# Attention between projections: TensorE's instructions queued in the order of the source

## The chip, the cores and the metric

The kernel runs on one core of a Trainium2 chip. A core has a matrix engine (TensorE, "PE" in the profile, with its weight loads listed apart as "PEld"), three engines for element-wise work (VectorE or DVE, ScalarE or ACT, GpSimd or POOL), a sync engine that issues transfers (SP) and 16 DMA engines. Each engine works through a queue of its own, and semaphores hold an instruction until what it needs is there. The metric is the time of one execution on the device, in microseconds (us). Lower is better.

## What is computed

One decoder layer over 1024 tokens of width 1024, in float32. What matters here is its first part: a projection of the normalized input feeds three groups of heads, of which the second is a "stick-breaking" attention with 8 heads of 64.

```python
hn = rms_norm(h, norm1_g[i])
proj = hn @ w_in[i]
a_b, a_c, a_h, q, k, v, c_u, c_v = jnp.split(proj, split_idx, axis=-1)
y_a = a_b * short_conv(a_c * a_h, conv_w[i])
q = rms_norm(q.reshape(bsz, s_len, ATTN_HEADS, HEAD_DIM), q_norm_g[i])
k = rms_norm(k.reshape(bsz, s_len, ATTN_HEADS, HEAD_DIM), k_norm_g[i])
y_b = stick_breaking_attention(q, k, v).reshape(bsz, s_len, ATTN_W)
...
h = h + jnp.concatenate([y_a, y_b, y_c], axis=-1) @ w_out[i]
```

and in the attention, for each block of 128 queries:

```python
z = jnp.einsum('bqhd,bkhd->bhqk', qi, kj) * scale
log_beta = jax.nn.log_sigmoid(z)
log_rem = jnp.where(causal, jax.nn.log_sigmoid(-z), 0.0)
suffix = lax.cumsum(log_rem, axis=3, reverse=True) - log_rem
weights = jnp.where(causal, jnp.exp(log_beta + suffix), 0.0)
o = jnp.einsum('bhqk,bkhd->bqhd', weights, vj)
```

A large feed-forward part and a gated embedding follow; they take most of the kernel's time, and the change does not touch them.

## The kernel before

**Precision.** A float32 product is made of three matmuls: each operand is split into a high part (a cast on ACT) and a low part (a subtraction on DVE or POOL), in `split` (L135). `product` (L161) issues high by high, high by low and low by high.

**Stages around the change.** First the gating projection and the projection of the first pair of heads run "alone". Then four rounds each weave one pair's attention with other matrix work: pairs 0, 1 and 2 with the projections of pairs 1, 2 and 3, and pair 3 with most of the convolution's products. The rest of the convolution, the output product `o_ps` and the feed-forward part follow.

**Pieces.** All this is written as Python generators that emit one piece of work and then yield its size in units:

- `project(pr)` (L343) goes over 8 row blocks t. A block takes 4 pieces of 6 matmuls with 384 columns into a bank of `ps_mm` (two banks); each piece counts 18 units. Then q, k and v are read out of the bank: squares on ACT (L374), a sum on DVE (L377), a power on POOL (L174), the scaled q and k on DVE (L382), and v in two parts on ACT and DVE (L141, L142) into a V tile. After two blocks, 72 units later, `turn_qk` (L393) transposes q and k (8 units). For the last two blocks of a pair this comes when the generator ends (alone) or in the loop ahead of the next weave.
- `stick(hh, g)` (L435), two pieces for blocks t = 2g and 2g+1: the scores z of 128 queries against all keys up to them, in one bank of `ps_z` (two banks) for t under 4 and in two from there on; two sigmoids on ACT read each bank (L454, L455); a scan over the row on DVE (L459) and a product with its result on DVE or POOL (L462) give the weights. A piece counts 2(t+1)+10 units.
- `gather(hh, g)` (L469): `turn(j)` transposes the weights of two key blocks for both query blocks (up to 4 transposes into a bank of `ps_tr`, 18 or 16 units), which ACT casts and DVE subtracts into `wT_hi` and `wT_lo`; a later piece (8 units) multiplies them with V into `av` (L502), high and low parts in turn. A turn runs up to two ahead of its product.

`attention()` (L525) goes through 8 steps of each pair: head 0 with g = 0 to 3, head 1 with g = 3 to 0. The scores of the next step are always emitted ahead of the gather of this one.

**Weaving.** `weave` (L267) takes the next piece from whichever of the two generators lags behind its share: 834 units of attention to 608 of projection in the first round, 808 to 608 in the second and third, 782 to 829 units of convolution (pieces of 12 units, three matmuls of 512 columns) in the last.

**What sets the order.** The order of emission is not yet the order in the queues. The framework plans all engines when the kernel is built (`schedule_with_timeline_sim=True`, L1339): it plays the program through on estimated times, and each engine takes, among the instructions that the estimate has ready, the one emitted first. TensorE may so issue a later piece while an earlier one is not ready in the estimate. On the chip each queue is then worked off in the order planned. Some places already fix an order by hand, with `tc.issue_after`, for transfers (L293, L334) and for matmuls late in the kernel.

**Tiles.** The tiles of heads (`QS`, `KH`, `KL`, `V`, `q_lo`) come from a pool of 56 slots (L25, L44), which also holds the 32 tiles of the normalized input. A new tile takes a slot only when all readers of an old one are done.

Of the kernel before, what the change touches and what calls it, by code (L numbers as in the profile page):

```python
# [13 lines left out]
P = 128  # L14
# [18 lines left out]
def hybrid_block(ctx: ExitStack, tc: tile.TileContext, a: dict):  # L33
# [5 lines left out]
    nc = tc.nc  # L39
# [60 lines left out]
    ones = const.tile([P, P], F32, name="ones")  # L100
# [5 lines left out]
    ident_r = const.tile([P, P], F32R, name="ident")  # L106
    ident = ident_r.bitcast(F32)
# [4 lines left out]
    below = const.tile([P, P], F32R, name="below")  # L112
# [17 lines left out]
    gk = load_const("gk", [P, 1])  # L130


    last_hi, last_power = [None], [None]

    def split(src, hi, lo, scale=None, low=nc.vector):  # L135
# [25 lines left out]
    def product(ps, terms, first=True, last=True):  # L161


        for i, ((lh, ll), (rh, rl)) in enumerate(terms):
            nc.tensor.matmul(ps, lh, rh, start=first and i == 0, stop=False)  # L165
            nc.tensor.matmul(ps, lh, rl, start=False, stop=False)  # L166
            done = nc.tensor.matmul(ps, ll, rh, start=False, stop=last and i == len(terms) - 1)  # L167
        return done

    def cols(parts, sl):  # L170
# [14 lines left out]
    def mean_square(acc, s):  # L185


        ps = bank(ps_tr, "ms_ps")
        for t in range(4):
            nc.tensor.matmul(ps[:, 2 * t:2 * t + 2], acc[:, t * P:(t + 1) * P], ones[:, :2],  # L190
                             start=True, stop=True)
        ms = small.tile([P, 4], F32, tag=f"ms{s}", name=name("ms"), bufs=1)
        nc.vector.tensor_scalar(out=ms, in0=ps.rearrange("p (t two) -> p t two", two=2)[:, :4, 0],
                                scalar1=1.0 / D, scalar2=EPS, op0=ALU.mult, op1=ALU.add)
        r = small.tile([P, 4], F32, tag=f"r{s}", name=name("r"), bufs=1)
        power_mhalf(r, ms, 4)
        return ms, r

    def spread(r, R):

        diag = slot("diag", shape=(P, 4, P))
        nc.vector.tensor_tensor(
            out=diag, in0=ident.unsqueeze(1).broadcast_to([P, 4, P]),
            in1=r.unsqueeze(2).broadcast_to([P, 4, P]), op=ALU.mult)
        ps = bank(ps_tr, "R_ps")
        nc.tensor.matmul(ps, ones, diag.rearrange("p t c -> p (t c)"), start=True, stop=True)
        nc.scalar.copy(R, ps)
        return R

# [57 lines left out]
    def weave(first, first_total, second, second_total):  # L267


        done = [0, 0]  # L270
        while True:
            if done[0] * second_total <= done[1] * first_total:
                got = next(first, None)
                if got is None:
                    return
                done[0] += got
            else:
                done[1] += next(second, 1000)

# [113 lines left out]
    def turn_qk(head, t, qk):  # L393

        QS, KH, KL, _, low_q = head
        th = t // 4
        tr = bank(ps_tr, "qk_tr")
        for i in range(2):
            for j in range(2):
                o = j * 256 + i * P  # L400
                nc.tensor.transpose(tr[:, o:o + P], qk[:, i, j * P:(j + 1) * P], ident)
        ws = slice((t % 4 - 1) * P, (t % 4 + 1) * P)

        split(tr[:, :256], QS[0][th][:, ws], low_q[th][:, ws], scale=gq)
        nc.scalar.activation(KH[0][th][:, ws], tr[:, 256:], AF.Copy, scale=gk)
        for hh, own in enumerate((lo_p, hi_p)):
            nc.vector.scalar_tensor_tensor(out=KL[hh][th][own, ws], in0=tr[own, 256:],
                                           scalar=gk[own], in1=KH[0][th][own, ws],
                                           op0=ALU.mult, op1=ALU.subtract)
# [11 lines left out]
    def attend(pr):  # L421

        QS, KH, KL, V, _ = heads[pr]
# [11 lines left out]
        def stick(hh, g):  # L435
            weights[hh, g] = []
            for t in (2 * g, 2 * g + 1):
                W = (t + 1) * P
                th, ts = block(t)

                rem = at.tile([P, T], F32, tag="rem", name=name("rem"), bufs=3)
                wt = at.tile([P, T], F32, tag="wt", name=name("wt"), bufs=4)
                for kh in reversed(range(th + 1)):
                    n = min(HT, W - kh * HT)
                    ks = slice(kh * HT, kh * HT + n)
                    z = bank(ps_z, "z")[:, :n]
                    nc.tensor.matmul(z, QS[hh][th][:, ts], KH[hh][kh][:, :n],
                                     start=True, stop=False)
                    nc.tensor.matmul(z, QS[hh][th][:, ts], KL[hh][kh][:, :n],
                                     start=False, stop=kh < th)  # L450
                    if kh == th:

                        nc.tensor.matmul(z[:, n - P:], ident_r, below, start=False, stop=True)
                    nc.scalar.activation(rem[:, ks], z, AF.Sigmoid, scale=-HD ** -0.5)  # L454
                    last_act[0] = nc.scalar.activation(wt[:, ks], z, AF.Sigmoid,  # L455
                                                       scale=HD ** -0.5)

                back = rem[:, :W][:, ::-1]
                nc.vector.tensor_tensor_scan(out=back, data0=back, data1=back, initial=1.0,  # L459
                                             op0=ALU.mult, op1=ALU.bypass)  # L460
                on_vector = t in (3, 5, 7)
                done = (nc.vector if on_vector else nc.gpsimd).tensor_tensor(  # L462
                    out=wt[:, :W - 1], in0=wt[:, :W - 1], in1=rem[:, 1:W], op=ALU.mult)
                if not on_vector:
                    last_pool[0] = done
                weights[hh, g].append(wt)
                yield 2 * (t + 1) + 10

        def gather(hh, g):  # L469
            own = slice(hh * HD, (hh + 1) * HD)  # L470
            wts = weights.pop((hh, g))
            av_of[0] ^= 1
            av = av_bank[:, av_of[0] * 256:(av_of[0] + 1) * 256]

            def turn(j):

                tr = bank(ps_tr, "w_tr")
                n = 0
                parts = []
                for kb in (2 * j, 2 * j + 1):  # L480
                    first = 0 if kb <= 2 * g else 1
                    parts.append((kb, n, first))
                    for i in range(first, 2):
                        nc.tensor.transpose(tr[:, n:n + P], wts[i][:, kb * P:(kb + 1) * P], ident)  # L484
                        n += P
                hi, lo = tmp("wT_hi", F32R), tmp("wT_lo", F32R)
                split(tr[:, :n], hi[:, :n], lo[:, :n])
                return parts, hi, lo, n // P

            turned = []  # L490
            for j in range(-2, g + 1):
                if j + 2 <= g:
                    turned.append(turn(j + 2))
                    yield 2 * turned[-1][3] + 10
                if j < 0:
                    continue
                parts, hi, lo, _ = turned.pop(0)
                for kb, o, first in parts:
                    m = 256 - first * P
                    lhs = V[kb // 2][:, kb % 2, hh].rearrange("p two d -> p (two d)")  # L500
                    for part in (hi, lo):
                        nc.tensor.matmul(av[:, first * P:], lhs, part[:, o:o + m],  # L502
                                         start=kb == 0 and part is hi,
                                         stop=kb == 2 * g + 1 and part is lo)
# [51 lines left out]
    def gating():  # L556
# [26 lines left out]
        def turn_c(th, j, yc, y):  # L583
            tr = bank(ps_tr, "c_tr")
            for t in range(4):
                nc.tensor.transpose(tr[:, t * P:(t + 1) * P],
                                    yc[:, t].rearrange("p g e -> p (g e)"), ident)
# [93 lines left out]
    for n in range(KT):  # L681
# [5 lines left out]
        for h in range(2):  # L687
            ps = wide_bank("pp_ps")
# [234 lines left out]
    for h in range(2):  # L923
        for n in (0, 4, 1, 5, 2, 6, 3, 7):
# [35 lines left out]
            j = n % 4  # L960
# [382 lines left out]
```

## Time and profile before

| | |
|---|---|
| median of 3 runs | 1221.15 us (1217.46 to 1222.93) |
| the profiled execution | 1216.81 us |
| its span on the core | 1214.9 us |
| mean granted TensorE clock | 0.993 |
| first and last score matmul (z) | 108.9 and 394.3 us from the span's start |
| first and last projection matmul (`qkv_ps`) | 75.3 and 318.1 us |

In the profile a line such as "L455 ACT ACTIVATE wt<-z 128x512 f32<-128x512 f32 x12 | 7.4, 619 | 0.0" is a group: source line, engine, operation, output and input by the program's names, shapes, the count, then busy us in total, the mean ns of one, and the idle time of the engine just before them. A table of stretches lists, for each stretch of the span, its length, and for PE, PEld, DVE, ACT and POOL the busy us with the number of instructions; then the granted TensorE clock as a share, the DMA engines' busy share and GB/s. A timeline row has start, duration, engine, line, operation and, in square brackets, how long the engine had been idle and on whom it waited. Matmuls overlap in the array, so their start-to-start distance, not their duration, is the time that each costs.

### The profile page before, as it was taken

The page shows a single profiled execution, that of the slowest core. Times are in us where ns is not written, and L with a number is a line of the kernel's source. Part 1 is how long each engine was busy: PE and PEld are TensorE (multiplying, and loading weights), DVE is VectorE, ACT ScalarE, POOL GpSimd, SP SyncE. Part 2 cuts the span into 40 slices and gives each one's busy share as a digit, 9 for nine tenths or more (in the row PEclk, how much of TensorE's full clock was granted, in tenths as well). Part 3 has the DMA queues.
Part 4 walks back from the last instruction along what each step waited for, and adds up shares of the span by engine and source line. Part 5 has one row for each costly group of instructions (what it writes and reads, how often), then busy time and mean ns, then how long its engine had stood idle before and what let it go on. Part 6 is the DMA issues. An engine that isn't in the chain of part 4 may idle for free.

```text
span 1214.9 us, 17743 instructions
## 1 busy us (share of the span) xinstructions
PE 1191.8 (98%) x5852; PEld 1018.2 (84%) x5852; DVE 886.8 (73%) x1310; ACT 629.1 (52%) x1244; POOL 400.9 (33%) x408
## 2 busy tenths in 40 slices
PE   9999899999999999999999999999999999999997
PEld 7899899898988888888888888888888888888886
DVE  7846888988887657877878768787665556753597
ACT  7736767667764355744333333356443444546542
POOL 3324345365343312124453544421023301013412
PEclk9999999999999999999999999999999999999998
DMA  9602359999554786779999899778889985654857
GB/s 318 222 18 94 124 166 267 247 184 171 132 116 101 164 287 207 198 194 269 251 256 251 231 261 258 217 249 277 321 248 313 279 264 171 217 163 112 179 160 208
DMA packets 127964, 254.04 MB, mean 209 GB/s; under 512 B 14496, under 2 KB 22432, under 8 KB 127168
## 3 DMA queue, kind: packets, MB, share of 16 engines
q1 hardware_dynamic: 94992, 168.08, 41.8%
q0 software_dynamic: 27664, 57.05, 25.0%
q10 hardware_dynamic: 5216, 27.79, 6.4%
q8 instruction: 46, 0.75, 0.2%
q14 instruction: 46, 0.38, 0.1%
HBM read 192.30 MB, written 92.80 MB: 235 GB/s over the span
## 4 chain that ended last, share of the span: by engine, by line
PE 86%; DVE 5%; DMA 4%; POOL 1%; issue 1%; ACT 1%; SPq 0%; ACTq 0%; DVEq 0%; POOLq 0%
PE f_ps L812 25%; PE d_ps L812 25%; PE g_ps L812 6%; PE qkv_ps L165 3%; PE qkv_ps L166 3%; PE qkv_ps L167 3%; PE av L502 2%; PE w_tr L484 2%; DVE rem L459 1%; PE vu_ps L167 1%; PE vu_ps L166 1%; PE vu_ps L165 1%; PE o_ps L167 1%; PE o_ps L165 1%; PE o_ps L166 1%
## 5 line engine op out<-in xcount | busy, mean ns | idle before, releaser
L139 DVE TENSOR_TENSOR w_lo<-raw,w_hi 128x512 fp32r<-128x512 f32 x280 | 245.1, 879 | 88.1 <-ACT w_hi L138 86.4
L138 ACT CAST w_hi<-raw 128x512 fp32r<-128x512 f32 x280 | 171.9, 619 | 232.6 <-PE d_ps L812 112.6
L812 PE MATMUL f_ps<-hn_hi,w_hi 128*128 128x512 f32 x448 | 175.1, 392 | 0.0
L812 PE MATMUL d_ps<-f_hi,w_hi 128*128 128x512 f32 x448 | 174.8, 390 | 0.0
L812 PE MATMUL f_ps<-hn_lo,w_hi 128*128 128x512 f32 x448 | 174.7, 390 | 0.0
L812 PE MATMUL f_ps<-hn_hi,w_lo 128*128 128x512 f32 x448 | 174.5, 390 | 0.0
L812 PE MATMUL d_ps<-f_hi,w_lo 128*128 128x512 f32 x448 | 174.3, 389 | 0.0
L812 PE MATMUL d_ps<-f_lo,w_hi 128*128 128x512 f32 x448 | 174.3, 389 | 0.0
L459 DVE TENSOR_TENSOR_SCAN rem<-rem 128x128 f32<-128x128 f32 (+3 forms) x64 | 90.2, 1420 | 23.0 <-ACT rem L454 22.9
L812 PEld LDWEIGHTS f_ps<-hn_lo,w_hi 128*128 128x128 f32 x448 | 84.4, 188 | 17.9 <-issue 0.2
L812 PEld LDWEIGHTS f_ps<-hn_hi,w_hi 128*128 128x128 f32 x448 | 84.5, 189 | 17.6 <-issue 0.2
L812 PEld LDWEIGHTS f_ps<-hn_hi,w_lo 128*128 128x128 f32 x448 | 84.4, 188 | 17.7
L812 PEld LDWEIGHTS d_ps<-f_hi,w_hi 128*128 128x128 f32 x448 | 84.1, 188 | 17.7 <-issue 0.2
L812 PEld LDWEIGHTS d_ps<-f_lo,w_hi 128*128 128x128 f32 x448 | 84.1, 188 | 17.6 <-issue 0.2
L812 PEld LDWEIGHTS d_ps<-f_hi,w_lo 128*128 128x128 f32 x448 | 84.1, 188 | 17.5
L165 PE MATMUL qkv_ps<-whi,xn_hi 128*128 128x384 f32 x256 | 90.4, 353 | 0.1
L167 PE MATMUL qkv_ps<-whi,xn_lo 128*128 128x384 f32 x256 | 87.8, 343 | 0.0
L166 PE MATMUL qkv_ps<-wlo,xn_hi 128*128 128x384 f32 x256 | 87.6, 342 | 0.0
L139 DVE TENSOR_TENSOR f_lo<-raw,f_hi 128x512 fp32r<-128x512 f32 x112 | 77.0, 718 | 12.6 <-ACT f_hi L138 12.2
L138 ACT CAST f_hi<-raw 128x512 fp32r<-128x512 f32 x112 | 67.0, 620 | 28.9 <-DMA raw<-f_dram 25.9
L798 POOL TENSOR_TENSOR S<-S,sq 128x512 f32<-128x512 f32 x19 | 27.4, 1440 | 157.8 <-ACT sq L874 157.8
L174 POOL TENSOR_TENSOR rs<-ss,mhalf 128x4 f32<-128x4 f32 x32 | 40.1, 1253 | 83.1 <-DVE ss L377 83.1
(252 smaller groups left out, 2704.4 us busy)
## 6 DMA issues: line engine op xcount, KB each, us to landing
raw<-in_w_ff SPq DMA_DIRECT2D x148, 256.0 KB, 4.1
raw<-f_dram SPq DMA_DIRECT2D x112, 256.0 KB, 5.1
raw<-w_sums SPq DMA_DIRECT2D x64, 256.0 KB, 3.9
f_dram<-f SPq DMA_DIRECT2D x48, 256.0 KB, 4.0
f_dram<-t SPq DMA_DIRECT2D x48, 256.0 KB, 3.7
w_sums<-in_w_ff POOLq DMA_DIRECT2D x8, 1024.0 KB, 11.6
w_sums<-w_sums POOLq DMA_DIRECT2D x8, 1024.0 KB, 13.0
raw<-in_w_out SPq DMA_DIRECT2D x28, 256.0 KB, 3.9
```

The costliest lines, as they stand in the source:

```text
L138: last_hi[0] = nc.scalar.copy(hi, src)
L139: low.tensor_tensor(out=lo, in0=src, in1=hi, op=ALU.subtract)
L165: nc.tensor.matmul(ps, lh, rh, start=first and i == 0, stop=False)
L166: nc.tensor.matmul(ps, lh, rl, start=False, stop=False)
L167: done = nc.tensor.matmul(ps, ll, rh, start=False, stop=last and i == len(terms) - 1)
L174: last_power[0] = nc.gpsimd.tensor_tensor(out=out, in0=in_, in1=mhalf[:, :n], op=ALU.pow)
L459: nc.vector.tensor_tensor_scan(out=back, data0=back, data1=back, initial=1.0, op0=ALU.mult, op1=ALU.bypass)
L484: nc.tensor.transpose(tr[:, n:n + P], wts[i][:, kb * P:(kb + 1) * P], ident)
L502: nc.tensor.matmul(av[:, first * P:], lhs, part[:, o:o + m], start=kb == 0 and part is hi, stop=kb == 2 * g + 1 and part is lo)
L798: return eng.tensor_tensor(out=out, in0=x, in1=y, op=ALU.add)
L812: done = nc.tensor.matmul(bank, l, r, start=first and k == 0 and i == 0, stop=k == len(b) - 1 and i == 2, skip_group_check=True)
```

## The change

The matmuls and transposes of the front part go through two small helpers that remember the last one emitted, and each turn of `weave` runs inside `tc.issue_after` with it. That call adds an edge of issue order, without a semaphore: each instruction that the block emits on the same engine (TensorE) is placed in the queue behind the remembered one. It does not wait for the end of that instruction, and instructions on other engines get no edge. The helpers replace `nc.tensor.matmul` and `nc.tensor.transpose` in `product`, `mean_square`, `spread`, `turn_qk`, `stick`, `gather` and `turn_c`; only the pieces that `weave` takes are put in order.

```diff
+    last_mm = [None]
+
+    def matmul(*args, **kw):
+        last_mm[0] = nc.tensor.matmul(*args, **kw)
+        return last_mm[0]
+
+    def transpose(*args):
+        last_mm[0] = nc.tensor.transpose(*args)
...
         for i, ((lh, ll), (rh, rl)) in enumerate(terms):
-            nc.tensor.matmul(ps, lh, rh, start=first and i == 0, stop=False)
-            nc.tensor.matmul(ps, lh, rl, start=False, stop=False)
-            done = nc.tensor.matmul(ps, ll, rh, start=False, stop=last and i == len(terms) - 1)
+            matmul(ps, lh, rh, start=first and i == 0, stop=False)
+            matmul(ps, lh, rl, start=False, stop=False)
+            done = matmul(ps, ll, rh, start=False, stop=last and i == len(terms) - 1)
...
         done = [0, 0]
         while True:
-            if done[0] * second_total <= done[1] * first_total:
-                got = next(first, None)
-                if got is None:
-                    return
-                done[0] += got
-            else:
-                done[1] += next(second, 1000)
+            with tc.issue_after(last_mm[0].ins):
+                if done[0] * second_total <= done[1] * first_total:
+                    got = next(first, None)
+                    if got is None:
+                        return
+                    done[0] += got
+                else:
+                    done[1] += next(second, 1000)
...
-                nc.tensor.transpose(tr[:, o:o + P], qk[:, i, j * P:(j + 1) * P], ident)
+                transpose(tr[:, o:o + P], qk[:, i, j * P:(j + 1) * P], ident)
```

The other places change in the same way.

More of the change, by code (lines that the diff above doesn't have):

```diff
@@ L189, in mean_square @@
         for t in range(4):
-            nc.tensor.matmul(ps[:, 2 * t:2 * t + 2], acc[:, t * P:(t + 1) * P], ones[:, :2],
+            matmul(ps[:, 2 * t:2 * t + 2], acc[:, t * P:(t + 1) * P], ones[:, :2],
                              start=True, stop=True)
@@ L205, in spread @@
         ps = bank(ps_tr, "R_ps")
-        nc.tensor.matmul(ps, ones, diag.rearrange("p t c -> p (t c)"), start=True, stop=True)
+        matmul(ps, ones, diag.rearrange("p t c -> p (t c)"), start=True, stop=True)
         nc.scalar.copy(R, ps)
@@ L446, in stick @@
                     z = bank(ps_z, "z")[:, :n]
-                    nc.tensor.matmul(z, QS[hh][th][:, ts], KH[hh][kh][:, :n],
+                    matmul(z, QS[hh][th][:, ts], KH[hh][kh][:, :n],
                                      start=True, stop=False)
-                    nc.tensor.matmul(z, QS[hh][th][:, ts], KL[hh][kh][:, :n],
+                    matmul(z, QS[hh][th][:, ts], KL[hh][kh][:, :n],
                                      start=False, stop=kh < th)
                     if kh == th:
-                        nc.tensor.matmul(z[:, n - P:], ident_r, below, start=False, stop=True)
+                        matmul(z[:, n - P:], ident_r, below, start=False, stop=True)
                     nc.scalar.activation(rem[:, ks], z, AF.Sigmoid, scale=-HD ** -0.5)
@@ L483, in turn @@
                     for i in range(first, 2):
-                        nc.tensor.transpose(tr[:, n:n + P], wts[i][:, kb * P:(kb + 1) * P], ident)
+                        transpose(tr[:, n:n + P], wts[i][:, kb * P:(kb + 1) * P], ident)
                         n += P
@@ L501, in gather @@
                     for part in (hi, lo):
-                        nc.tensor.matmul(av[:, first * P:], lhs, part[:, o:o + m],
+                        matmul(av[:, first * P:], lhs, part[:, o:o + m],
                                          start=kb == 0 and part is hi,
@@ L585, in turn_c @@
             for t in range(4):
-                nc.tensor.transpose(tr[:, t * P:(t + 1) * P],
+                transpose(tr[:, t * P:(t + 1) * P],
                                     yc[:, t].rearrange("p g e -> p (g e)"), ident)
```

## The prediction

> **What bounds the kernel now.** I read the page's shares first, then tables of busy time by stretch over the part that the change touches, then the order of TensorE's matmuls there.
>
> ```profile
> span 1214.9 us, 17743 instructions
> PE 1191.8 (98%) x5852; PEld 1018.2 (84%) x5852; DVE 886.8 (73%) x1310; ACT 629.1 (52%) x1244; POOL 400.9 (33%) x408
> ```
>
> TensorE (PE) bounds the whole. Its busy time is modelled and covers short gaps, so for attention I read PEld, the weight loads: each matmul has its own, and where nothing is late they fill the time. In the table the columns are PE, PEld, DVE, ACT, POOL, granted clock. The first three rows are the three weaves with projections 1, 2 and 3, the fourth the weave with the convolution; then one packed stretch, then three poor ones.
>
> ```profile
> 111.00:175.50 64.50, 60.32 (x376) 57.15 (x375) 55.66 (x83) 44.98 (x115) 26.10 (x26) 0.97 0.48 162
> 175.50:245.50 70.00, 67.31 (x438) 64.59 (x437) 59.71 (x91) 49.03 (x125) 37.19 (x37) 0.98 0.89 235
> 245.50:318.50 73.00, 69.42 (x459) 66.20 (x458) 63.80 (x103) 51.64 (x131) 40.65 (x40) 1.00 0.83 160
> 318.50:408.50 90.00, 88.12 (x482) 73.55 (x480) 64.64 (x89) 45.44 (x103) 35.95 (x31) 1.00 0.60 131
> ...
> 151.00:175.50 24.50, 24.50 (x160) 24.22 (x160) 21.47 (x32) 14.95 (x37) 6.08 (x6) 0.95 0.52 178
> ...
> 140.00:151.00 11.00, 8.13 (x49) 6.15 (x48) 10.52 (x15) 9.91 (x24) 5.26 (x5) 0.97 0.01 1
> 210.00:221.00 11.00, 8.31 (x47) 6.76 (x46) 10.46 (x13) 9.24 (x24) 8.61 (x8) 0.89 0.83 144
> 279.00:289.00 10.00, 7.21 (x45) 5.30 (x44) 9.13 (x13) 9.36 (x23) 7.93 (x7) 1.00 0.81 138
> ```
>
> Weight loads fill 24.22 of 24.5 us in the packed stretch. In the first three weaves they are idle for 7.35, 5.41 and 6.80 us, 19.6 us in all, and the three poor stretches hold 4.85 + 4.24 + 4.70 = 13.8 us of it. There DVE is 91 to 96% busy and ACT 84 to 94%: attention runs alone and its vector work sets the pace. The projections' own matmuls in these stretches show why.
>
> ```profile
> 111.00:140.00 29.00, 21.78 (x114) 19.20 (x112) 3.47 (x9) 3.48 (x9) 1.00 0.63 209
> 140.00:151.00 11.00, 0.00 (x0) 0.01 (x1) 1.01 (x3) 0.64 (x2) 0.97 0.01 1
> 210.00:221.00 11.00, 1.57 (x5) 1.64 (x6) 1.03 (x3) 1.15 (x3) 0.89 0.83 144
> 279.00:289.00 10.00, 0.12 (x1) 0.15 (x2) 0.98 (x3) 0.76 (x2) 1.00 0.81 138
> ```
>
> The order is not the source's. Projection 1 races ahead (114 matmuls in 29 us) and then issues none in 11 us, with its first four row blocks done and the fifth not begun. Its next matmul starts at 151.06, right after two late evictions:
>
> ```profile
> 146.93 0.64 ACT L141 ACTIVATE V<-qkv_ps,r 128x128 fp32r<-128x128 f32 x2
> ...
> 150.26 0.61 DVE L142 SCALAR_TENSOR_TENSOR V<-qkv_ps,r,V 128x128 fp32r<-128x128 f32 x2
> ```
>
> Those free the two `ps_mm` banks. I read them as late because the V tiles need slots of the 56 that attention's first head still held; the rows show the lateness, not the slot.
>
> **The change part by part.** It adds no operation and no wait on another engine. It fixes TensorE's order in the four weaves: a piece's matmuls go in only after the last matmul of the piece emitted before. No DMA, ACT, DVE, POOL or SP instruction gets an edge.
>
> *Removed.* The first projection piece of row block 4 is then emitted about half-way through a weave (288 of 608 units), some 13 us of TensorE work behind the first head's last score. The blocked stretch should go. Ceiling: 19.6 us less the roughly 1% of idle that a packed stretch keeps, 2 us, gives 17.5. The convolution weave adds 90 - 88.12 = 1.9. The clock adds a little:
>
> ```profile
> 152.16 0.52 PE L165 MATMUL qkv_ps<-whi,xn_hi 128*128 128x384 f32 x1
> 152.48 0.52 PE L166 MATMUL qkv_ps<-wlo,xn_hi 128*128 128x384 f32 x1
> ...
> 155.14 0.33 PE L166 MATMUL qkv_ps<-wlo,xn_hi 128*128 128x384 f32 x1
> 155.32 0.33 PE L167 MATMUL qkv_ps<-whi,xn_lo 128*128 128x384 f32 x1
> ```
>
> After the poor stretch 384-column matmuls start 0.32 us apart instead of 0.17. A granted 0.95 over 24.5 us is 1.2 us, and 0.89 over 11 us is 1.2 us: 2.4 us. In all 17.5 + 1.9 + 2.4 = **21.8 us to gain**.
>
> *Added: waits with no filler.* What is queued behind a waiting matmul is now everything else on TensorE. To find the waits I lay out the source order (S: scores of one block, P: six projection matmuls, T: transposes, A: weights times V) and compare TensorE's own time between two dependent pieces with the chain on the other engines. Start-to-start times:
>
> ```profile
> 140.33 0.39 PE L449 MATMUL z<-KL,QS 128*128 128x512 f32 x1
> 140.56 0.22 PE L453 MATMUL z<-below,ident 128*128 128x128 f32 x1
> 140.62 0.45 PE L447 MATMUL z<-KH,QS 128*128 128x512 f32 x1
> ...
> 142.16 0.27 PE L502 MATMUL av<-wT_lo,V 128*128 128x256 f32 x1
> 142.27 0.28 PE L502 MATMUL av<-wT_hi,V 128*128 128x256 f32 x1
> 142.39 0.60 PE L401 MATMUL qk_tr<-ident,qk 128*128 128x128 f32 x4
> 142.75 0.36 PE L502 MATMUL av<-wT_lo,V 128*128 128x256 f32 x1
> ```
>
> That is 0.23 for 512 columns, 0.17 for 384 (above), 0.12 for 256, 0.06 for 128, and 0.36 for four transposes. So P is 1.04, S of block 7 0.97, S of block 6 0.86, A at most 0.47. The chains, from the second weave's groups (mean ns behind the comma):
>
> ```profile
> L455 ACT ACTIVATE wt<-z 128x512 f32<-128x512 f32 x12 | 7.4, 619 | 0.0
> L455 ACT ACTIVATE wt<-z 128x384 f32<-128x384 f32 x4 | 2.0, 509 | 0.0
> L138 ACT CAST wT_hi<-w_tr 128x512 fp32r<-128x512 f32 x12 | 7.0, 596 | 1.9 <-PE w_tr L484 1.9
> L459 DVE TENSOR_TENSOR_SCAN rem<-rem 128x1024 f32<-128x1024 f32 x2 | 5.0, 2475 | 0.0
> L459 DVE TENSOR_TENSOR_SCAN rem<-rem 128x768 f32<-128x768 f32 x2 | 3.5, 1756 | 2.3 <-ACT rem L454 2.3
> L459 DVE TENSOR_TENSOR_SCAN rem<-rem 128x512 f32<-128x512 f32 x2 | 2.4, 1204 | 0.0
> L139 DVE TENSOR_TENSOR wT_lo<-w_tr,wT_hi 128x512 fp32r<-128x512 f32 x12 | 7.9, 681 | 0.6 <-ACT wT_hi L138 0.4
> ```
>
> (1) Score banks. `ps_z` has two; each is read by two sigmoids. S6, P, S7: the second bank of S6 is free 0.41 + 0.2 + 2 x 0.51 + 2 x 0.62 = 2.9 us after S6 begins; TensorE wants it at 0.87 + 1.04 + 0.52 = 2.4. Wait 0.5, twice in a weave, and by the same working 0.25 for the S4, S5 pair: 1.5 us a weave if ACT does nothing else. ACT is 49.03 of 70 us busy, half of that not sigmoids, so a pair's 2.9 us meet some 1 us of other work: 5 us a weave. I take 3, nearer the free case.
>
> (2) First product of a gather. Each gather is emitted right behind a pair of scores, whose scans DVE then works through; the low parts of the first transposes stand behind the second scan. From S5's end: 0.2 + 1.24 + 1.76 + 0.68 + 0.2 = 4.1 us, and TensorE comes to A's low part after P, T, T, P, 2.8 us: wait 1.3. After S7: 4.8 against 4.2 or 4.3, 0.6 and 0.5. After S3: 3.4 against 2.45, 0.95. The rest about 0.4. That is 3.8 us a weave with an empty queue. DVE is 85% busy; one more operation of 0.7 us ahead at each of eight gathers makes it 9.4. I take 5, nearer the bound that has rows.
>
> (3) Last turn of q and k. The transposes of row blocks 6 and 7 are emitted between weaves, and the next piece stands behind them. Their chain:
>
> ```profile
> L374 ACT ACTIVATE qk_sq<-qkv_ps 128x256 f32<-128x256 f32 x8 | 3.1, 387 | 1.0 <-PE qkv_ps L167 0.9
> L377 DVE TENSOR_REDUCE ss<-qk_sq 128x4 f32<-128x260 f32 x9 | 3.7, 414 | 0.8 <-ACT qk_sq L374 0.8
> L382 DVE TENSOR_TENSOR qk<-qkv_ps,rs 128x256 f32<-128x256 f32 x8 | 3.3, 419 | 1.7 <-POOL rs L174 1.6
> ...
> L174 POOL TENSOR_TENSOR rs<-ss,mhalf 128x4 f32<-128x4 f32 x9 | 12.1, 1344 | 22.3 <-DVE ss L377 22.3
> ```
>
> 0.39 + 0.41 + 1.34 + 0.42 and 0.5 for the steps between is 3.1 us. Before the first weave nothing stands between: 3.1. Before the second there are 1.6 us of work: 1.5, of which 0.4 is already in (2). Later ones have 3.3 or more: none. Sum 4.2, between 2 and 6.
>
> Three weaves of 3 + 5 give 24 (16 to 43). The convolution weave has shorter filler pieces but a freer DVE (64.64 of 90): 4 to 8 by the same chains, less what its wider spacing covers; I take 3, from 1 to 8. **Added: 24 + 3 + 4.2 = 31 us** (19 to 57). The net is 31 - 22 = +9 us, with bounds -3 and +35.
>
> ```profile
> 141.82 0.39 PE L502 MATMUL av<-wT_lo,V 128*128 128x256 f32 x1 [0.41 <-DVE wT_lo L139]
> ...
> 150.29 1.11 PE L484 MATMUL w_tr<-ident,wt 128*128 128x128 f32 x4 [1.14 <-DVE KL L407]
> ```
>
> These are two of today's waits (in brackets, us). In the first nothing overtook the low product that stood waiting. [...] If matmuls could overtake, (1) to (3) would cost nothing and the net would be -22.
>
> The profiled execution took 1216.8 us, span 1214.9; the median shown is 4.3 above it. Plus 9 gives 1226 against the profile and **1230** against the median.
>
> **The rivals.** *Faster.* The low parts go ahead of the scans in DVE's queue, and ACT keeps the sigmoids together: (2) vanishes, (1) is 1.5 a weave, and what is added falls to 4.5 + 4.2 + 1 = 10: -12 us, 1209. For it: the plan orders ACT and DVE anew, and the three poor stretches are dear. Against it: the scans are emitted first, and DVE has 63.8 us of work for the third weave's 66 of weight loads. *Even.* Waits of 22 pay back just what is won: 1221. That the order does not move at all is excluded by the x0 row. *A DVE queue one deep.* The high ends hold for (1) and (2): 43 + 3 + 4 - 22 = +28, 1249. It decides from the point at which DVE's backlog lasts from one gather to the next; 59.71 of 70 us is near it. *Clock.* The new waits of a step fall close together and halve the clock as in the 152.16 row. Each such window costs 1.2 us by the granted clock; 12 pairs of long scores (four in each of three weaves) add 14 to the forecast: 1244. [...]
>
> **How the numbers follow.** Forecast, slower by 9: 0.45. Faster: 0.23. Even: 0.19. DVE queue: 0.09. Clock: 0.04. The likeliest case alone spans 1222 to 1240. To leave out no more than 2 in 10 the range reaches over most of the faster case and to the middle of the DVE one: **1207 to 1249**. A measurement here tells about 0.5%, 6 us, from no change. Faster by more than that 0.23; within it, the even case and the forecast's low edge, 0.27; slower 0.50.
>
> **What would show it.** Right on the removal: no stretch of 10 us in 111 to 318 without projection matmuls, weight loads evenly filled. Right on the cost: in the table of waits, products waiting for `wT_lo` and scores for `wt` go from a few to dozens, together over 15 us; a 2 to 3 us wait of the q and k transposes near 115 to 120. Wrong, if those stay under 10 us together (then 1209 to 1221), or if waits of projections for weights or V appear, for which I found no reason. After attention nothing should move.

## The result and the profile after

| | before | after |
|---|---|---|
| median | 1219.31 us (1216.32 to 1222.93, 4 runs) | 1268.55 us (1267.53 to 1270.20, 4 runs) |
| span of the profiled execution | 1214.9 us | 1267.7 us |
| mean granted TensorE clock | 0.993 | 0.981 |

The ratio is 1.0404, with an interval of 1.0369 to 1.0439: **slower by 4%**. One run in this document is left out of its median and ratio, one of the four of `e1_products_loose`, 1992.6 us at a granted clock of 0.555; as it was the profiled one, that experiment has times but no trace to compare. The shares on the page of the changed kernel:

```profile
PE 1210.2 (95%) x5852; PEld 1031.2 (81%) x5852; DVE 905.5 (71%) x1310; ACT 635.7 (50%) x1244; POOL 402.8 (32%) x408
```

Every engine has as many instructions as before; lines have moved down by some 11 (the scan L459 is L470, the product L462 is L473, the low part L139 is L149). To find the place of the 52.8 us I divided both spans at the same work: at the first projection matmul of pairs 1, 2 and 3 (the three weaves), at the end of the last projection (the convolution weave), and at the first output product `o_ps`. The table of stretches of the kernel before (length, then PE, PEld, DVE, ACT, POOL, granted clock, DMA share, GB/s):

```profile
115.70:183.90 68.20, 64.11 (x409) 61.19 (x410) 58.31 (x88) 47.56 (x121) 30.42 (x31) 0.97 0.53 167
183.90:251.60 67.70, 65.01 (x421) 62.28 (x420) 57.52 (x87) 47.17 (x120) 34.40 (x36) 0.97 0.88 236
251.60:318.10 66.50, 62.92 (x412) 59.80 (x411) 58.48 (x92) 45.83 (x117) 34.90 (x33) 1.00 0.86 167
318.10:420.30 102.20, 99.73 (x533) 82.89 (x532) 76.77 (x107) 52.09 (x116) 41.44 (x36) 1.00 0.60 130
```

and of the kernel after:

```profile
118.80:198.20 79.40, 69.49 (x420) 65.31 (x420) 61.56 (x85) 49.38 (x122) 29.64 (x31) 0.94 0.40 127
198.20:278.60 80.40, 70.38 (x424) 66.27 (x423) 62.00 (x88) 49.46 (x121) 33.10 (x33) 0.94 0.78 201
278.60:356.90 78.30, 67.45 (x409) 62.69 (x408) 62.85 (x91) 47.23 (x117) 34.22 (x34) 0.96 0.73 137
356.90:470.90 114.00, 102.55 (x533) 84.34 (x532) 81.78 (x112) 53.28 (x116) 43.81 (x36) 0.98 0.59 128
```

Behind the last row of each, 794.6 us are left before and 796.8 after. The three weaves grew from 202.4 to 238.1 us. In them weight loads were idle for 7.01 + 5.42 + 6.70 = 19.1 us before and are idle for 14.09 + 14.13 + 15.61 = 43.8 us after. Matmuls (the PE column, whose ends are modelled) were idle for 10.4 us and are idle for 30.8 us. About as many loads (1251 recorded, 1241 before) are also busy for longer, 194.3 us against 183.3, at a granted clock of 0.94, 0.94 and 0.96 where it had been 0.97, 0.97 and 1.00. Beside the forecast, whose terms I spread over the same places:

| place | forecast | measured |
|---|---|---|
| before the first weave | +3.1 | +3.1 |
| three weaves, loads idle (7.6 = 24 + 1.1 - 17.5) | +7.6 | +24.7 |
| three weaves, loads busy for longer (clock) | -2.4 | +11.0 |
| convolution weave up to `o_ps` | +1.1 | +11.8 |
| the rest | 0 | +2.2 |
| sum | +9.4 | +52.8 |

The removal did happen. The projection's own matmuls in a stretch that had none before:

```profile
139.00:151.00 12.00, 5.96 (x27) 4.73 (x26) 0.72 (x2) 1.16 (x3) 0.90 0.12 22
```

The longest gap between projection matmuls inside a weave is now 6.6 us, from 148.0 to 154.6, where three gaps of 9.8 to 11.7 us stood before.

What came instead of those stretches stands in the table of TensorE's waits after (who waited for whom: us in total, times, longest):

```profile
PE av L136 <- DVE wT_lo L149: 23.8, 25, 2.1
PE qk_tr L140 <- DVE qk L393: 5.4, 3, 3.8
PE o_ps L136 <- DVE cv_acc L672: 5.3, 1, 5.3
PE w_tr L140 <- DVE wT_lo L149: 4.0, 2, 2.4
PE qk_tr L140 <- DVE wT_lo L149: 2.8, 2, 2.2
...
PE z L136 <- ACT wt L466: 0.4, 1, 0.4
```

Waits of products for the low parts went from 1.6 us in 3 to 23.8 us in 25:

```profile
PE av L502 <- DVE wT_lo L139: 1.6, 3, 0.9
```

One of them in the timeline after (start, duration, engine, line, operation, idle time before). L470 is the scan, L473 the product of weights and scan, L149 the low part:

```profile
132.30 1.31 POOL L473 TENSOR_TENSOR wt<-wt,rem 128x639 f32<-128x639 f32 x1 [2.37 <-DVE rem L470]
132.59 2.64 DVE L470 TENSOR_TENSOR_SCAN rem<-rem 128x768 f32<-128x768 f32 x1 [0.22 <-ACT rem L465]
...
134.59 0.28 PE L136 MATMUL av<-wT_hi,V 128*128 128x256 f32 x1
135.34 0.96 DVE L473 TENSOR_TENSOR wt<-wt,rem 128x767 f32<-128x767 f32 x1
136.21 1.15 DVE L149 TENSOR_TENSOR wT_lo<-w_tr,wT_hi 128x512 fp32r<-128x512 f32 x2
136.95 0.39 PE L136 MATMUL av<-wT_lo,V 128*128 128x256 f32 x1 [2.08 <-DVE wT_lo L149]
...
137.83 0.49 PE L136 MATMUL qkv_ps<-whi,xn_hi 128*128 128x384 f32 x1
138.11 0.52 PE L136 MATMUL qkv_ps<-wlo,xn_hi 128*128 128x384 f32 x1
138.43 0.52 PE L136 MATMUL qkv_ps<-whi,xn_lo 128*128 128x384 f32 x1
```

The high part goes into the array at 134.59; the low part, next in the queue, stands until 136.95, because DVE first works off the scan and also the product L473. Projection matmuls that need neither stand behind it, and when they come they start 0.28 and 0.32 us apart, where 0.17 is usual: the granted clock from 139 to 141 us is 0.50.

The scan itself is long, 2.64 us. Before, the same scan of block 5 met no work on POOL:

```profile
131.03 1.59 POOL L462 TENSOR_TENSOR wt<-wt,rem 128x639 f32<-128x639 f32 x1
134.13 1.76 DVE L459 TENSOR_TENSOR_SCAN rem<-rem 128x768 f32<-128x768 f32 x1 [2.22 <-ACT rem L454]
...
143.28 2.29 DVE L459 TENSOR_TENSOR_SCAN rem<-rem 128x1024 f32<-128x1024 f32 x1
```

After, POOL's product runs from 132.30 to 133.61 and the scan, put down as started at 132.59, takes 0.88 us longer, for 1.02 us of overlap. With block 7 it is the same, 1.46 us longer than the scan of 2.29 above for an overlap of 1.61:

```profile
238.44 1.77 POOL L473 TENSOR_TENSOR wt<-wt,rem 128x895 f32<-128x895 f32 x1 [3.61 <-DVE rem L470]
238.60 3.75 DVE L470 TENSOR_TENSOR_SCAN rem<-rem 128x1024 f32<-128x1024 f32 x1 [0.34 <-ACT rem L465]
```

The groups by form show it as a mean over attention (110 to 470 us; busy us, mean ns), here for block 7, before:

```profile
L459 DVE TENSOR_TENSOR_SCAN rem<-rem 128x1024 f32<-128x1024 f32 x8 | 21.1, 2642 | 0.0
```

and after:

```profile
L470 DVE TENSOR_TENSOR_SCAN rem<-rem 128x1024 f32<-128x1024 f32 x8 | 28.4, 3547 | 2.1 <-ACT rem L465 2.1
```

### The profile page after: what moved, and what is told of

Its sections match the earlier page's. It is cut to its first block, busy times and chain, and to the rows that moved or that the text cites. A ratio compares the mean times of both kernels' runs of the same rounds, so it can differ in the third digit from the quotient of the medians.

```text
span 1267.7 us, 17707 instructions
## 1 busy us (share of the span) xinstructions
PE 1210.2 (95%) x5852; PEld 1031.2 (81%) x5852; DVE 905.5 (71%) x1310; ACT 635.7 (50%) x1244; POOL 402.8 (32%) x408
## 4 chain that ended last, share of the span: by engine, by line
PE 65%; DVE 2%; POOL 1%; DMA 1%; issue 0%; ACT 0%; POOLq 0%
PE f_ps L823 24%; PE d_ps L823 24%; PE o_ps L136 7%; PE g_ps L823 6%; PE cv_ps L136 2%; DVE rem L470 1%; PE ms_ps L898 1%; PE av L136 0%; DMA u_sums<-u_sums 0%; POOL cv_u L660 0%; PE z L136 0%; POOL cv_acc L670 0%; PE w_tr L140 0%; PE R_ps L913 0%; DMA u_sums<-in_w_ff 0%
## 5 line engine op out<-in xcount | busy, mean ns | idle before, releaser
L149 DVE TENSOR_TENSOR w_lo<-raw,w_hi 128x512 fp32r<-128x512 f32 x280 | 253.5, 909 | 90.2 <-ACT w_hi L148 84.2
L470 DVE TENSOR_TENSOR_SCAN rem<-rem 128x128 f32<-128x128 f32 (+3 forms) x64 | 101.9, 1603 | 25.4 <-ACT rem L465 24.9
L136 PE MATMUL qkv_ps<-whi,xn_hi 128*128 128x384 f32 x256 | 94.1, 368 | 0.0
L149 DVE TENSOR_TENSOR f_lo<-raw,f_hi 128x512 fp32r<-128x512 f32 x112 | 77.2, 719 | 10.1 <-ACT f_hi L148 9.7
L473 POOL TENSOR_TENSOR wt<-wt,rem 128x127 f32<-128x127 f32 (+4 forms) x40 | 50.6, 1269 | 89.0 <-DVE rem L470 56.5
```

The lines of the kernel that those rows point to most:

```text
L136: last_mm[0] = nc.tensor.matmul(*args, **kw)
L149: low.tensor_tensor(out=lo, in0=src, in1=hi, op=ALU.subtract)
```

## The experiments

The theory: each step's first weights-times-V products wait for low parts that stand behind DVE's scans, and everything queued behind them waits too. The rivals are the waits of the transposes of q and k; the lost clock by itself; and a cost of keeping order at all, wherever it is loosened. All ratios are against the kernel before, at 1217.1 to 1217.8 us in these batches.

| run | what | median us | ratio (interval) |
|---|---|---|---|
| e1_products_loose | products may be overtaken | 1232.29 | 1.0119 (1.0101 to 1.0137) |
| e2_qk_loose | q and k transposes may be overtaken | 1267.39 | 1.0408 (1.0389 to 1.0427) |
| e3_both_loose | both | 1230.19 | 1.0101 (1.0083 to 1.0120) |
| e4_rounds_0_2 | order in the three weaves alone | 1256.65 | 1.0321 (1.0302 to 1.0341) |
| e5_round_3 | order in the convolution weave alone | 1229.71 | 1.0091 (1.0060 to 1.0122) |
| e6_mult_on_pool | 24 products moved from DVE to POOL | 1246.24 | 1.0236 (1.0211 to 1.0261) |
| e7_window_3 | order with a window of 3 pieces | 1238.44 | 1.0169 (1.0142 to 1.0196) |
| e7_window_6 | window of 6 | 1214.13 | 0.9982 (0.9961 to 1.0002) |
| e7_window_12 | window of 12 | 1221.32 | 1.0032 (1.0016 to 1.0049) |
| e9_window_6_qk | window of 6, q and k loose | 1214.39 | 0.9971 (0.9957 to 0.9985) |
| e8_v_own_pool | kernel before, one V tile in slots of its own | 1215.77 | 0.9985 (0.9968 to 1.0002) |
| e10_filler | kernel after, 128 idle-time matmuls added | 1267.66 | 1.0400 (1.0367 to 1.0432) |

### Which matmuls hold the queue: e1, e2, e3

```diff
-                        matmul(av[:, first * P:], lhs, part[:, o:o + m],
+                        nc.tensor.matmul(av[:, first * P:], lhs, part[:, o:o + m],
```

A product that isn't remembered has nothing queued behind it.

> The weights-times-V products stay behind the piece ahead of them, but nothing is queued behind them any more. Theory A (products that wait for their low parts hold up everything behind them: 23.8 us of waits in the changed kernel, and half-rate clock after them): 1268 falls by 25 to 35, to 1233 to 1243, and the waits of products on wT_lo fall under 8 us. Theory B (DVE's backlog is the bound, the product is only where it shows): the waits move to transposes and scores, and the time stays at 1258 or above.

Measured: 1232.29, 36 us less than the kernel after with one word changed. That products hold up what is queued behind them carries most of the loss. How far their own waits fell isn't shown, as this run has no trace to compare; e3 below, where they are loose too, shows 8.3 us. The same for q and k:

```diff
-                transpose(tr[:, o:o + P], qk[:, i, j * P:(j + 1) * P], ident)
+                nc.tensor.transpose(tr[:, o:o + P], qk[:, i, j * P:(j + 1) * P], ident)
```

> Only the transposes of q and k are let go: nothing is queued behind them. Theory A: their waits in the changed kernel (5.4 on qk, 2.8 on wT_lo) and the half-rate clock after the first of them go, 6 to 10 us: 1259 to 1263. If the three us before the first weave are merely paid at the next piece: within 3 us of 1268.

Measured: 1267.39, 1 us less, within what the runs of either kernel spread. The wait has only moved on to the scores that need those transposes, as the table of waits of this run shows:

```profile
PE av L136 <- DVE wT_lo L149: 25.1, 27, 2.1
PE z L136 <- DVE QS L427: 7.4, 3, 3.5
```

With both loose:

> Products and q and k transposes both let go; scores, weight transposes and projections keep the source's order. Theory A: the gains add, 1225 to 1235. If the removal of the blocked stretches is worth what the prediction said (some 20 us), this order has few waits and could come below the kernel before: 1205 to 1219. Theory B: 1255 or above.

Measured: 1230.19, still 1% above the kernel before. Its waits for the low parts:

```profile
PE av L513 <- DVE wT_lo L149: 8.3, 7, 2.0
```

Its three weaves, in the table of stretches:

```profile
114.30:186.70 72.40, 66.30 (x413) 63.29 (x414) 59.59 (x89) 49.58 (x124) 29.70 (x32) 0.95 0.46 148
186.70:260.10 73.40, 66.38 (x425) 63.28 (x424) 59.31 (x87) 47.60 (x120) 35.11 (x36) 0.95 0.85 223
260.10:332.40 72.30, 65.44 (x414) 62.56 (x414) 60.57 (x92) 46.83 (x118) 31.33 (x33) 0.95 0.79 154
```

They are 15.7 us longer than before, with loads idle for 29.0 us and the clock at 0.95 in each. Products that may be overtaken still leave the transposes and scores of the next step in order; that these are what is left of the loss was not tested by itself.

### Where: e4, e5

```diff
-            with tc.issue_after(last_mm[0].ins):
+            with tc.issue_after(last_mm[0].ins) if rounds[0] in ORDERED else nullcontext():
...
+        rounds[0] = pr
         weave(attending, ATTEND + {0: AHEAD, 3: -AHEAD}.get(pr, 0), fill,
```

with `ORDERED` as (0, 1, 2) and as (3,).

> The source's order in the three weaves with projections alone; the convolution's weave is left to the plan. From the two traces: the first weave lost 20 us, the second 12, the third 7, together 39; the fourth with the end of the convolution 13. So 1219 + 39 = 1258 if the losses are local, 1268 if the late attention costs the fourth weave as much in any order.

> The source's order in the convolution's weave alone. If the losses are local: 1219 + 13 = 1232, of it 5.3 us of wait of the output product for the convolution's last piece and the half-rate clock after it. If that end was late only because the weaves before were: 1222 to 1226.

Measured: some 39 us over the kernel before with order in the three weaves, some 12 in the convolution weave. Their sum is about the whole, so the losses are local to the weaves. In e5 a wait stands out that the kernel after has too:

```profile
PE o_ps L136 <- DVE cv_acc L672: 5.2, 1, 5.2
```

It is a wait of the output product for the convolution's last element-wise steps. Its place in the timeline of the kernel after:

```profile
465.26 0.39 PE L136 MATMUL cv_ps<-xn_hi,wlo 128*128 128x512 f32 x1
466.06 3.96 POOL L670 TENSOR_TENSOR cv_acc<-cv_acc,R 128x512 f32<-128x512 f32 x1
...
470.06 0.69 DVE L672 TENSOR_TENSOR cv_acc<-cv_ps,cv_acc 128x512 f32<-128x512 f32 x1 [1.16 <-POOL cv_acc L670]
470.90 0.77 PE L136 MATMUL o_ps<-y_hi,wo_hi 128*128 128x512 f32 x1 [5.25 <-DVE cv_acc L672]
```

and before:

```profile
420.32 0.47 PE L165 MATMUL o_ps<-y_hi,wo_hi 128*128 128x512 f32 x1 [0.62 <-DVE cv_acc L661]
```

After the last convolution matmul at 465.26 TensorE stands until 470.90, mostly for POOL's step of 3.96 us. Before, the wait was 0.62. Loose products remove it: e3's stretch from the last projection to `o_ps` has no such wait.

### What DVE does in that time: e6

```diff
-                on_vector = t in (3, 5, 7)
+                on_vector = False
```

The 24 products L473 that stood between scans and low parts go to POOL.

> Strict order as in the change, with the 24 products of weights and remainders that DVE did (0.7 to 1.8 us each) moved to POOL. In the trace of the change DVE works on a scan and on such a product between a turn's transposes and its low part. Theory (what stands ahead on DVE makes the products wait): waits of products on wT_lo fall from 24 us to about 15, time 1250 to 1260. Rival (POOL's longer products slow DVE's scans, or come late for the transposes): 1265 to 1285.

Measured: 1246.24, 22 us less than the kernel after, more than I expected. Waits for the low parts fall to 14.4 us, though the scans of block 7 stay long, with all the products L473 now on POOL (a mean of 3496 ns where the kernel after has 3547):

```profile
PE av L136 <- DVE wT_lo L149: 14.4, 18, 1.5
```
```profile
L470 DVE TENSOR_TENSOR_SCAN rem<-rem 128x1024 f32<-128x1024 f32 x8 | 28.0, 3496 | 0.4 <-ACT rem L465 0.2
```

So what stands ahead of the low parts in DVE's queue sets the wait, and L473, which the prediction had left out of that chain, is a large part of it. With shorter waits for the low parts, waits of scores for the sigmoids show up, 2.3 us in 5 where the kernel after has 0.4 in 1:

```profile
PE z L136 <- ACT wt L466: 2.3, 5, 1.1
```

### How much order: the windows, e7 and e9

```diff
+            behind.append(last_mm[0])
-            with tc.issue_after(last_mm[0].ins):
+            with tc.issue_after(behind[max(0, len(behind) - 6)].ins):
```

Each piece is now queued behind the piece 3, 6 or 12 turns back, and may pass the ones between.

> Each piece is queued behind the last matmul of the piece emitted three before it, not of the one just before. Theory (strict order has no filler for a chain of some 4 us; three pieces are about 2 us of matmuls): about half of the products' waits go, 1235 to 1245. Rival (any fixed order loses, since the plan's estimate is better informed): above 1250.

> The same with six pieces, about 4 us of matmuls, as long as the chain. Theory: waits of products under 6 us; the blocked stretches stay away, since the projection can run ahead by a few pieces only: 1205 to 1222. Rival: above 1240.

> The same with twelve pieces, about 8 us. Before the change the projection ran ahead by some 5 us before it was blocked, so such a window hardly binds: the order and time of the kernel before, 1214 to 1222, with its three stretches without projection matmuls back.

Measured: 1238.44, 1214.13 and 1221.32. At 3 the products still wait for 12.4 us in all. At 12 two of the three blocked stretches come back, in the second and third weave, as gaps of 9.4 us between projection matmuls. At 6 there is no gap over 4 us inside a weave, and products wait for 2.3 us in all; its three weaves:

```profile
118.70:182.30 63.60, 63.32 (x411) 61.28 (x411) 55.24 (x83) 47.45 (x119) 29.26 (x29) 0.97 0.47 153
182.30:250.20 67.90, 64.99 (x426) 61.81 (x425) 59.54 (x90) 47.65 (x122) 37.38 (x36) 1.00 0.92 239
250.20:315.80 65.60, 63.13 (x416) 60.50 (x415) 58.32 (x89) 45.59 (x116) 35.65 (x33) 1.00 0.88 169
```

That is 197.1 us against 202.4 before, with loads idle for 13.5 us and matmuls for 5.7. In this run the scans of blocks 7 and 5 average 2381 and 1820 ns again. Its largest wait left is that of the q and k transposes, ahead of the first weave, so I loosened those too:

```profile
PE qk_tr L140 <- DVE qk L394: 4.2, 2, 3.8
```

> Window of six pieces, and nothing is queued behind the transposes of q and k. In the window of six alone the largest wait left is 4.2 us on qk, 3.8 of it before the first weave, with half-rate clock after it. If that is local, both go: 1214 less 4 to 6, 1207 to 1211, clear of the kernel before. If it is merely paid at the next score (as with strict order, where letting them go won 1 us): 1212 to 1215.

Measured: 1214.39 in 12 runs, ratio 0.9971 (0.9957 to 0.9985): the only one whose interval lies wholly below the kernel before, but no better than the window alone. The wait of 4.2 us is gone from its table and, other than in e2, no wait of the scores has come in its place (0.5 us for `QS`); where the gain went was not found. It is 0.3% below the kernel before.

### Why the stretches had been empty: e8

The prediction had read that V tiles waited for slots. Here, in the kernel before, the second V tile of each pair (row blocks 2 and 3, whose late evictions held the two banks) has slots of its own; two rings are made smaller to make room.

```diff
-STAGES = 7
-WBUFS = 20
+STAGES = 6
+WBUFS = 18
...
+    vx = front.enter_context(tc.tile_pool(name="vx", bufs=2))
...
-                V[t // 2] = slot("V", F32R, (P, 2, 2, 2, HD))
+                V[t // 2] = (vx.tile([P, 2, 2, 2, HD], F32R, tag="vx", name=name("V")) if t == 2
+                             else slot("V", F32R, (P, 2, 2, 2, HD)))
```

> The kernel before, with the second V tile of each pair in a pool of its own, so that it needs none of the 56 slots (two fewer weight buffers and one fewer stage pay for the room). If the missing slot for that tile stopped the projection after four row blocks (96 matmuls), it now goes on to six (144) or is not stopped at all. If something else stopped it, the stretch of 10 us without projection matmuls stays where it was, after 96. Time 1210 to 1225 either way.

Measured: 1215.77, and the time is not the point. Projection matmuls of the kernel before, then of this run, up to their stop and in the gap behind it:

```profile
115.70:139.15 23.45, 18.46 (x96) 16.44 (x96) 2.71 (x7) 2.25 (x6) 1.00 0.77 257
139.15:151.00 11.85, 0.24 (x2) 0.01 (x1) 1.01 (x3) 1.02 (x3) 0.97 0.01 1
```
```profile
118.10:161.55 43.45, 27.92 (x144) 24.77 (x144) 4.13 (x11) 3.76 (x10) 1.00 0.36 116
161.55:169.35 7.80, 0.25 (x2) 0.19 (x1) 0.67 (x2) 0.91 (x3) 0.90 0.84 286
```

A row block has 24 such matmuls. The stop has moved from behind four blocks to behind six, in each of the three weaves. So the slot of that V tile was what blocked. That the new stop is the same wait of the next V tile (blocks 4 and 5), which still takes a common slot, follows by analogy only.

### The clock, and the room in the waits: e10

```diff
                 parts, hi, lo, _ = turned.pop(0)
+                if j == 0 and g < 2:
+                    for _ in range(8):
+                        matmul(av, ident_r, xn[0][0][0][:, :256], start=True, stop=True)
```

The added matmuls write a bank that the next product overwrites. There are 128, at 0.12 us some 15 us of TensorE's time.

> Strict order as in the change, with eight extra matmuls of 256 columns (about 0.95 us) ahead of the first product of each of the 16 gathers with g = 0 or 1, written where the product then starts anew. 15 us of work is added, most of it inside waits (18 us by the trace of the change). If only the waits count: 1266 to 1271. If the half-rate clock after the waits costs some 15 us on top: some of its windows go, 1256 to 1264. If the extra work is paid in full: 1280 or above.

Measured: 1267.66, the time of the kernel after with some 15 us more work for TensorE. Waits for the low parts fall from 23.8 us to 17.9, so part of the work went into them; the rest is not accounted for one by one, as the clock changed too. The third weave of this run:

```profile
281.00:357.50 76.50, 66.93 (x433) 62.81 (x432) 63.23 (x91) 46.95 (x116) 33.70 (x34) 1.00 0.74 138
```

It has a full clock where the kernel after has 0.96, and it is 1.8 us shorter, of the 11.8 us by which that weave had grown. So a full clock does not bring the time back there; the added work in this weave may hide some of what it is worth. Over whole runs (granted clock of a run, its time):

```
e10_filler      0.987 1269.31    0.988 1268.21    0.991 1267.12    0.995 1263.29
kernel before   0.989 to 0.991: 1220.5 (mean of 7 runs)    0.995 and 0.996: 1215.4 (mean of 15 runs)
```

A lower clock does go with a longer run, by about 5 us for 0.005 to 0.006. The kernel after, whose four runs all lie between 0.981 and 0.985, is some 0.010 under the kernel before; by that slope the lost clock goes with some 9 us of its 49, an estimate. In e10 the run with the lowest clock and that with the highest differ by 6 us (1269.31 less 1263.29), and the one at 0.995 is still 47.1 us above the mean of the 8 runs of the kernel before with that clock (1216.16). That run carries the added work too, and it is one run: it shows that the loss does not vanish at a full clock, not how much of the 47.1 are waits.

## Why the prediction was right in sign and wrong in size

**Removal: right in kind, too large in size.** The order was moved, projection matmuls come into the stretches that were empty, and the slot behind them is shown by e8. The signs that the prediction asked for came: no such stretch of 10 us, products' waits over 15 us, a wait of the q and k transposes just ahead of the first weave; only the even filling of weight loads did not. But the 17.5 us took nearly all idle time of weight loads, 19.6 us, as time to be won. Matmuls were idle for 10.4 of it only. In the kernel before, in the kernel after and in e7 with 6 pieces, loads are idle for 8.7, 13.0 and 7.8 us more than matmuls, so that part stayed in all three. What causes it is open. The run with a window of 6, which has neither the gaps nor many waits, gives an idea of what was to be had: 5.6 us of the loads' idle time and 5.3 us of the three weaves' length.

**Score banks (1): wrong.** The prediction took 3 us a weave, 9 in all. After, scores wait for the sigmoids once, for 0.4 us. My reading is that TensorE reaches the banks late anyway, since it has already stood for the low parts. That e6, with shorter waits for those, shows 2.3 us in 5 fits it: waits in one queue don't simply add up.

**First product of a gather (2): the mechanism right, the size wrong, and this is the first step that failed.** The prediction worked out 3.8 with an empty queue and 9.4 with a busy one, and took 5 a weave "nearer the bound that has rows". Waits for low parts in the three weaves (the table of waits after, from 118.8 to 356.9 us):

```profile
PE av L136 <- DVE wT_lo L149: 18.7, 19, 2.1
```

With the two rows of transposes above (4.0 and 2.8) that is 25.5 us, 8.5 a weave, near its high end, where 15 had been taken. In the wait that it had priced at 1.3, the one of the timeline above, 2.08 us were measured: the chain lacked L473 (0.96 us) and had the scan at its duration of before, when nothing ran beside it (1.76, where 2.64 came). The steps between engines in its sums, 0.2 us each here and in (1) and 0.5 in all in (3), were my estimates and stand in no row; in that wait the product starts 0.06 us after the end of the low part that it needs (136.21 and 0.68, then 136.95). e6 shows that what stands in DVE's queue sets these waits, and e1 that products which hold the queue are most of the 49 us.

**What a wait costs: the second step that failed.** Waits were priced at their own length. All waits together came out near the forecast: matmuls are idle for 30.8 us in the three weaves, where 24 + 1.1 had been added. But e1 gives back 36 us, where products' waits were 23.8 us in all, and e6 22 us for 9.4 us less of them. In the three weaves the forecast is missed most by what no single wait shows: idle time of loads beyond that of matmuls, 13.0 us where the ceiling had left 2, and loads that take 11.0 us longer where 2.4 had been booked as won.

**Idle time and clock: a gain was booked, a loss came.** The prediction booked 2.4 us of clock as won. It gave the rival "Clock" 0.04 and "A DVE queue one deep" 0.09, each by itself; something of both came in one run. Loads idle for 24.7 us more and busy for 11.0 us longer make up the 35.7 us of the three weaves. By the slope above some 9 us of the whole loss go with the clock; no run here varied the clock alone, so its share stays an estimate.

**Last turn of q and k (3): right in place, without effect.** Ahead of the first weave stand 3.8 us of wait and 3.1 us of time, as worked out. But e2 gives back only 1 us: in it the scores wait for the same chain, 7.4 us for `QS`.

**Convolution weave: wrong.** I took 3 us, from 1 to 8, less 1.9 to gain. It grew by 11.8. Of this 4.6 us is the growth (from 0.62 to 5.25) of a wait that the prediction didn't look for, `o_ps` for the convolution's last element-wise work, and 5.1 us are products waiting for low parts:

```profile
PE av L136 <- DVE wT_lo L149: 5.1, 6, 1.6
```

That is the row of the window from 356.9 to 475 us. The prediction's last sentence said that nothing moves after attention; the wait for `o_ps` is just where attention ends.

**The range.** Its upper bound, 1249, is the rival with a DVE queue one deep: the high ends of (1) and (2), middle values for the rest, and all of the 22 us as gain. Even the high ends of everything, +35 to the median of before, end at 1256. None of these joined what came together: less to gain than 22 us, scans that take longer beside POOL's products (2.91 to 3.86 us for block 7, where the kernel before has 2.29 without a product beside the scan), and a clock that falls (0.981 after 0.993). The case "Faster" needed the low parts ahead of the scans in DVE's queue; the timeline shows them behind.

## What to carry to other kernels

An order that is written strictly makes each wait of one piece a wait of all; a window keeps the far racing ahead away and lets near pieces fill in. Of 3, 6 and 12 pieces 6 did best here, by my estimate about as long as the longest chain between two dependent pieces (some 4 us); even so it won only about 0.3%. When such a chain is priced, count all that its engine does between, and take durations under the overlap that the new order brings, not those of the old trace. Price a wait at more than its length: letting go the products won 36 us here, where their waits had been 23.8. And don't take all idle time of weight loads as gain: the part that lay under running matmuls stayed here in each order.

## What the runs showed of the hardware

Scans on DVE that began while POOL was running a product of weights and scan took longer by about their overlap with it: two of them by 0.88 us for an overlap of 1.02, and by 1.46 for 1.61. All eight scans of 1024 in the kernel after began so, with overlaps of 0.76 to 1.72 us, and took 2.91 to 3.86 us. Of the eight of the kernel before, three began so, with overlaps of 0.49 to 0.52, and took 2.63 to 2.66; three met no product of POOL on wide tiles and took 2.29. In all eleven, what goes beyond 2.29 is 0.14 or 0.15 us less than the overlap. The other two lie beside another product of POOL, L649. The one at 350.17, with a product of 1.87 us put down 0.04 us behind its start, took 4.07; the one at 363.98, wholly under a product put down at 363.65 for 3.66 us (its mean in the kernel after is 1.35), took 2.27. So not every product that the trace puts beside a scan goes with a longer scan; which of the two waits, and for what, is not settled here.

The clock fell after short waits. No wait of TensorE inside the three weaves was longer than 2.4 us (that of 3.8 stands just ahead of the first), and they were granted 0.94, 0.94 and 0.96, where the kernel before had 0.97, 0.97 and 1.00. Behind the wait of 2.08 us that ended at 136.95, 384-column matmuls started 0.28 and then 0.32 us apart from 137.83 on, where 0.17 is usual. In the kernel before, such matmuls started 0.32 us apart behind a wait of 1.14 us that ended at 150.29, at a granted clock of 0.58 from 152 to 154 us. What share of idle time within which stretch lowers the clock stays open: no run here varied it by itself.
